# One-hot rows compared from PSUM, weight low parts all on GpSimd, 72 instead of 56 early chunks, and gathered rows paced into the last group

## The chip, the cores and the metric

One core of a Trainium2 chip runs one launch of the kernel. The metric is the device time of that launch in microseconds (us), the median of the runs shown; lower is better. The engines are TensorE (PE; PEld is its weight load), VectorE (DVE), ScalarE (ACT), GpSimd (POOL) and the DMA queues, which SyncE (SP), ACT and POOL issue. TensorE has a granted clock with two levels, 2.4 GHz (1.0 in the profile) and 1.2 GHz (0.5).

## The reference

One decoder layer on 512 tokens of width 2048: pooling mixer and dilated attention, cross attention over 256 memory tokens, then the part that this change is mostly about, PEER, a product-key mixture of 16384 single-neuron experts:

```
q = hf @ w_pq                                  # 8 heads x 2 halves of 128
s1, s2 = halves of q against 128 sub-keys each
v1, i1 = top_k(s1, 16);  v2, i2 = top_k(s2, 16)
sc, ci = top_k(all sums v1 + v2, 16)           # 16 of 256 candidates
experts = i1[ci // 16] * 128 + i2[ci % 16];  gates = softmax(sc)
a = hf . w_u[experts];  y = sum over experts of gates * gelu(a) * w_v[experts]
out = rmsnorm(x + y)
```

## The kernel before, in words

**Precision.** Each f32 weight tile of 128x1024 is split into two fp32r parts: a high part `wh` (a cast on ACT, L143) and a low part `wl = raw - wh` (L144, on DVE or on POOL, by the argument `lo_eng`). Three matmuls (`mm3`, L150 to L152) make one product. Both parts have three buffers, the raw tile four.

**Two ways through PEER.** For the last 320 tokens all 16384 experts are computed densely, as 128 chunks of 128 experts; a matrix of gates, zero where an expert was not picked, multiplies them. For the first 192 tokens only the picked experts' rows are gathered: 128 tokens ("dot0", "axpy0", 128 rows each) and 64 middle tokens (packed as 2x64, "dot1", "axpy1", 64 rows each). Each row is one indirect DMA on POOL (L114; 128 partitions x 8 KB, 1 MB) and one DVE operation over 2048 elements with the other operand or the sum in PSUM. These 389 steps stand in one list; `behind(n)` pops n of them at a time, `n` being a rate (`RATE`) per chunk. Row buffers are four at most in the stages of interest.

**Stages from the pick on.** (a) The pick, for three blocks of 128 tokens (`pick_steps`, L263): candidate sums, top 16, and per head a one-hot over 50 candidates for 16 slots: compare (L293), multiply by the expert number (L295), reduce (L296), all on DVE. Its result is transposed by PE (L1054 to L1056) into `e12T` and `gT`. After each block `a_until` computes seven early chunks of h @ w_u with a gelu; they go to DRAM (`gad`). (b) The gates: for four tokens at a time (80 blocks), `gates` makes two one-hots of 128 (L1114), multiplies one by the gate (L1116), one PE product per token makes the 128x128 gate matrix (L1119), ACT copies it to a 2 MB stage (L1120). These run between early chunks 21 to 55. (c) The 16 groups of 8 chunks, each 16 output tiles `dd` of 24 matmuls: group g multiplies the gated chunks with w_v and adds to `xT` (L1193), while `c_chunk` makes the 8 chunks of the next group. The 9 late groups (chunks 56 to 127) compute their chunks there; the 7 early groups come last and load theirs from DRAM.

```
1023        lo = G if j < RB * KB else (V, G) if j < K1 else G if j < K1 + GRP or j % 2 == 0 else V
1053            pt = pa.tile([P, 512], F32, name="pa")
1054            TE.transpose(pt[:, 0:P], e12[:, 0, :], ident)
1061            a_until(KB * b + KB)
1114            V.tensor_tensor(u, iota.unsqueeze(1).unsqueeze(1).broadcast_to([P, 2, 4, P]),
1115                            e12T[:, :, t:t + 4].unsqueeze(3).broadcast_to([P, 2, 4, P]), op=ALU.is_equal)
1116            V.tensor_tensor(u[:, 1], u[:, 1], gT[:, t:t + 4].unsqueeze(2).broadcast_to([P, 4, P]), op=ALU.mult)
1117            pg = pa.tile([P, 4, P], F32, name="pa")
1119                TE.matmul(pg[:, j], u[:, 0, j], u[:, 1, j], start=True, stop=True)
1120            S.copy(stage[:, :, t4 * 4:t4 * 4 + 4].rearrange("p e t -> p t e"), pg)
```

**What sets the order.** A scheduler orders each engine's instructions ahead of time by priority and its own time model; an engine then runs them strictly in that order. POOL follows the program's order from the gates on (L1065). `issue_after` keeps a gathered row behind the last DVE split (`anchor`, L159). In PSUM the pool `pa` has two banks.

**Earlier.** Attention begins (L753 on) with the rotary tables: positions are loaded, `trig` makes `sinT` and `cosT` (L764 to L767), and `rope` (L771) applies them to each head's q and k on POOL.

Of the kernel before, what the change touches and what calls it, by code (L numbers as in the profile page):

```python
# [9 lines left out]
F32 = mybir.dt.float32  # L10
# [7 lines left out]
P = 128  # L18
# [3 lines left out]
KD = D // P  # L22
# [20 lines left out]

RATE = (3.0, 2.2, 2.5, 2.0, 0.25, 1.2)

# [3 lines left out]

K1, U0, GE = 56, 0, 2  # L50

KB = 7

# [10 lines left out]
def hybrid_kernel(ctx: ExitStack, tc: tile.TileContext, a: dict, out: bass.AP):  # L64
# [28 lines left out]
    r2c = const.tile([P, TR], F32, name="r2c")  # L93
    rz = const.tile([P, NB], F32, name="rz")[:, :RB]
    accx = const.tile([P, TR], F32, name="accx")
    xT = big.tile([P, KD, TR], F32, name="xT")
    x0 = big.tile([P, D], F32, name="x0")
# [37 lines left out]
    def load_w(src, lo_eng=None, parts=1):  # L135
# [11 lines left out]
        return wh, wl  # L147

    def mm3(ps, wh, wl, xh, xl, start, stop):
        TE.matmul(ps, wh, xh, start=start, stop=False)  # L150
        TE.matmul(ps, wh, xl, start=False, stop=False)  # L151
        TE.matmul(ps, wl, xh, start=False, stop=stop)  # L152

# [108 lines left out]

    def pick_steps(vals, inds, alloc, res):  # L263
        v1, v2 = vals[:, 0], vals[:, 1]
# [24 lines left out]
        eid = alloc([P, PH, 16], name="eid")  # L289
        ohs = [alloc([P, 16, NCAND], name="oh%d" % i) for i in range(2)]  # L290
# [15 lines left out]

    def pick(vals, inds, alloc):
        res = []
        for _ in pick_steps(vals, inds, alloc, res):
            pass  # L310
        return res
# [52 lines left out]
    v0 = kt.tile([P, HEADS, P], F32, name="v0")  # L364
    halo = kt.tile([P, 8, 16], F32, name="halo")

    def alloc_ma():
# [7 lines left out]
    with tc.tile_pool(name="ep", bufs=1) as ep, tc.manual_schedule(engines={mybir.EngineType.SP}):  # L375
# [269 lines left out]
        def xr_sq(k):  # L645
            sumsq(lambda n: ep.tile([P, TR], F32, name="jk", bufs=2), accx, xT[:, k, :], k == 0, TR)
# [63 lines left out]
        for k in range(KD):  # L710
            hooks_x[k // 8][k % 8] = [lambda k=k: xr_sq(k)]
        for g in range(4):
# [29 lines left out]
    def pick0():  # L742
        res = []
        yield from pick_steps(vals0, inds0, lambda shape, name, dt=F32: (mA if name in ("oh0", "oh1") else m2)(shape, dt=dt), res)
        V.tensor_copy(sidx, res[0])
        V.tensor_copy(sgate, res[1])
# [6 lines left out]
    with tc.tile_pool(name="ac", bufs=1, reuse_waits="tile") as ac, tc.tile_pool(name="at", bufs=2, reuse_waits="tile") as at:  # L753
        tmp2k = lambda n=TR, dt=F32: at.tile([P, T], dt, name="t2k", bufs=3)[:, :n]
        mask = ac.tile([P, T], F32, name="mask")
        nc.scalar.dma_start(mask, a["mask"])
        invf = ac.tile([32, 1], F32, name="invf")
        nc.scalar.dma_start(invf, a["invfreq"])
        cosT = ac.tile([32, TR], F32, name="cosT")
        sinT = ac.tile([32, TR], F32, name="sinT")  # L760
        posi = tmp2k(TR, I32)[:32]
        nc.scalar.dma_start(posi, a["positions"][:, T0:].broadcast_to([32, TR]))
        ang = tmp2k()[:32]
        V.tensor_copy(ang, posi)  # L764
        V.tensor_scalar(ang, ang, scalar1=invf, scalar2=None, op0=ALU.mult)
        trig(ang, tmp2k()[:32], sinT, cosT)
        V.tensor_scalar(sinT[0:16], sinT[0:16], scalar1=-1.0, scalar2=None, op0=ALU.mult)  # L767
        rx = r2c
# [252 lines left out]
    def a_chunk(j, stay=False):  # L1021

        lo = G if j < RB * KB else (V, G) if j < K1 else G if j < K1 + GRP or j % 2 == 0 else V
        ps = proj_one(a["w_u"][j], dH, dL, ND, lo_eng=lo, rate=RATE[4] if j < RB * KB else RATE[5] if j < K1 else 0)
# [12 lines left out]
    with tc.tile_pool(name="tw", bufs=1, reuse_waits="tile") as tw:  # L1037
        for b in range(RB):
            eidf, gtf = pick(vals[:, b], inds[:, b], lambda shape, name, dt=F32: tw.tile(shape, dt, name=name))
            ei = tw.tile([P, 2, PH * 16], I32, name="ei")  # L1040
# [13 lines left out]
            TE.transpose(pt[:, 0:P], e12[:, 0, :], ident)  # L1054
            TE.transpose(pt[:, P:2 * P], e12[:, 1, :], ident)
            TE.transpose(pt[:, 2 * P:3 * P], gtf, ident)  # L1056
# [37 lines left out]
    with tc.tile_pool(name="gw", bufs=2, side="right", reuse_waits="tile") as gw:  # L1094
        for k4 in range(4):
            pt = pa.tile([P, 512], F32, name="pa")
            for kk in range(4):
                k = 4 * k4 + kk
                hn = gw.tile([P, SG, NS], F32, name="hn0")
                for g in range(SG):  # L1100
                    V.scalar_tensor_tensor(out=hn[:, g, :], in0=xT[:, k, :NS], scalar=gains[:, 3, k:k + 1], in1=r2c[:, :NS], op0=ALU.mult, op1=ALU.mult)
                TE.transpose(pt[:, kk * P:(kk + 1) * P], hn.rearrange("p g t -> p (g t)"), ident)
            S.copy(hy1[:, k4 * 512:(k4 + 1) * 512], pt)

        stage = None

        def gates(i):
            nonlocal stage
            tb, t4 = divmod(i, 8)
            if t4 == 0:  # L1110
                stage = gw.tile([P, P, 32], F32, name="stage", bufs=1)
            u = gw.tile([P, 2, 4, P], F32, name="u", bufs=3)
            t = i * 4
            V.tensor_tensor(u, iota.unsqueeze(1).unsqueeze(1).broadcast_to([P, 2, 4, P]),  # L1114
                            e12T[:, :, t:t + 4].unsqueeze(3).broadcast_to([P, 2, 4, P]), op=ALU.is_equal)
            V.tensor_tensor(u[:, 1], u[:, 1], gT[:, t:t + 4].unsqueeze(2).broadcast_to([P, 4, P]), op=ALU.mult)  # L1116
            pg = pa.tile([P, 4, P], F32, name="pa")
            for j in range(4):
# [18 lines left out]
    with tc.tile_pool(name="vg", bufs=2, side="right", reuse_waits="tile") as vg, \  # L1137
# [30 lines left out]
        cs = []  # L1168
        slots = (NG - 1) * KD - 4
        n2 = NCH - K1  # L1170
# [3 lines left out]
        for jj in range(GRP):  # L1174
            cs.append(c_chunk(GRP * order[0] + jj))
            behind(RATE[5])
        fin = None
        for i, g in enumerate(order):
# [8 lines left out]
            for dd in range(KD):  # L1187
# [8 lines left out]
                behind(rate2 if i < n2 // GRP - 1 else rate3)  # L1196
                if last:
                    if dd == KD - 2:
                        S.activation(warm, accf[:, 0:1], AF.Sqrt)
                    sumsq(ftmp, accf, xT[:, dd, NS:], dd == 0, ND, eng=V)  # L1200
                    S.activation(xT[:, dd, NS:], xT[:, dd, NS:], AF.Copy, scale=gains[:, 4, dd:dd + 1])
            if i == NG - 2:
                behind(1000)
                for k4 in range(4):
                    pt = pa.tile([P, 512], F32, name="pa")
                    for kk in range(4):
                        TE.transpose(pt[:, kk * P:(kk + 1) * P], y1[0][:, (4 * k4 + kk) * P:(4 * k4 + kk + 1) * P], ident)
                    o = xT[:, 4 * k4:4 * k4 + 4, :NS]
                    for sg_ in range(SG):
                        V.tensor_tensor(o, pt.rearrange("p (k g t) -> p k g t", k=4, t=NS)[:, :, sg_, :], o, op=ALU.add)  # L1210
                for k in range(KD):
                    sumsq(ftmp, accs, xT[:, k, :NS], k == 0, NS)
                    S.activation(xT[:, k, :NS], xT[:, k, :NS], AF.Copy, scale=gains[:, 4, k:k + 1])
            cs = nxt
# [100 lines left out]
```

## Time and profile before

| | |
|---|---|
| three runs | 3178.96, 3163.85, 3175.17 us; median 3175.17 |
| the profiled execution | 3175.37 us, span 3173.6 us |
| mean granted clock | 0.968 |
| busy share of the span | PE 93%, DVE 76%, POOL 45%, ACT 41% |
| DMA | 912.79 MB, mean 288 GB/s |
| last gathered row issued | 3005 us into the span |

A busy PE is not a PE at its peak, since matmuls overlap; so PE's work is counted here in matmuls and their start-to-start time. All stretches are microseconds from the start of the span. The stage of picks, early chunks and gates lies at 1146 to 1690; the groups' windows, cut at the first addition of each group, run from 1749 to 3152.

### The profile page before, as it was taken

What the parts mean: (1) busy time and instruction counts of PE and PEld (TensorE: products, weight loads), DVE (VectorE), ACT (ScalarE), POOL (GpSimd) and SP (SyncE); (2) the same over time, 40 slices, a digit from 0 to 9 for tenths busy, and PEclk for the clock granted to TensorE, in tenths of its full rate; (3) what the DMA queues carried; (4) which work ended last, traced back from release to release, by engine and by line L of the source; (5) the groups of instructions that cost most, each with busy time, mean ns of one, the idle gap of its engine ahead of it and who ended that gap; (6) DMA issues with size and microseconds to landing.
All of it is one profiled execution on the core that took longest, in us unless ns stands there. A gap on an engine that the chain in (4) does not pass through costs nothing.

```text
span 3173.6 us, 47405 instructions
## 1 busy us (share of the span) xinstructions
PE 2947.7 (93%) x18311; PEld 2832.5 (89%) x18311; DVE 2422.7 (76%) x3360; ACT 1298.6 (41%) x1789; POOL 1433.8 (45%) x826
## 2 busy tenths in 40 slices
PE   7999879998988997899998999999999999999997
PEld 5868769988978997899998999999999999899997
DVE  7797877798878579599894767777777678787756
ACT  5676534432344443355543333333433333233334
POOL 0000046644534665544546555555555554454532
PEclk9999989999989998999999999999999999999998
DMA  7886737888975344588888989999899999999953
GB/s 261 295 300 214 244 119 282 330 309 339 342 266 192 111 127 124 182 302 318 315 304 315 357 325 359 357 367 355 330 372 353 353 354 358 346 357 362 343 163 106
DMA packets 243521, 912.79 MB, mean 288 GB/s; under 512 B 23488, under 2 KB 85600, under 8 KB 192224
## 3 DMA queue, kind: packets, MB, share of 16 engines
q1 hardware_dynamic: 136304, 471.21, 42.2%
q0 software_dynamic: 55296, 402.68, 32.1%
q10 hardware_dynamic: 51696, 35.88, 3.7%
q8 instruction: 144, 2.36, 0.3%
q14 instruction: 81, 0.66, 0.1%
HBM read 874.22 MB, written 35.45 MB: 287 GB/s over the span
## 4 chain that ended last, share of the span: by engine, by line
PE 66%; DVE 20%; DMA 5%; issue 5%; ACT 2%; POOL 0%; ACTq 0%; POOLq 0%; DVEq 0%; SPq 0%
PE pm L150 11%; PE pm L152 11%; PE pm L151 11%; PE pa L152 9%; PE pa L150 9%; PE pa L151 9%; DVE wl L144 2%; DVE u L1114 2%; DVE oh L295 1%; DVE oh L293 1%; PE pm L400 1%; PE pm L401 1%; PE pm L399 1%; PE pa L1119 1%; DMA rows<-in_w_v_rows_dram,sidx 1%
## 5 line engine op out<-in xcount | busy, mean ns | idle before, releaser
L144 POOL TENSOR_TENSOR wl<-wraw,wh 128x1024 fp32r<-128x1024 f32 x369 | 930.5, 2526 | 1433.3 <-ACT wh L143 1401.4
L143 ACT ACTIVATE wh<-wraw 128x1024 fp32r<-128x1024 f32 (+1 forms) x658 | 693.7, 1058 | 1042.1 <-PE pm L151 467.0
L152 PE MATMUL pa<-ch,wl 128*128 128x320 f32 x2048 | 634.5, 312 | 25.4 <-DVE wl L144 23.5
L150 PE MATMUL pm<-dH,wh 128*128 128x320 f32 x2048 | 640.4, 313 | 15.0 <-DVE cl L1164 6.5
L152 PE MATMUL pm<-dH,wl 128*128 128x320 f32 x2048 | 640.6, 313 | 6.1 <-DVE wl L144 3.9
L150 PE MATMUL pa<-ch,wh 128*128 128x320 f32 x2048 | 636.7, 311 | 7.3 <-DVE xT L1193 4.7
L151 PE MATMUL pm<-dL,wh 128*128 128x320 f32 x2048 | 639.0, 312 | 0.0
L151 PE MATMUL pa<-cl,wh 128*128 128x320 f32 x2048 | 635.3, 310 | 0.0
L144 DVE TENSOR_TENSOR wl<-wraw,wh 128x1024 fp32r<-128x1024 f32 (+1 forms) x289 | 377.4, 1308 | 166.5 <-ACT wh L143 158.7
L152 PEld LDWEIGHTS pa<-ch,wl 128*128 128x128 f32 x2048 | 387.1, 189 | 30.4 <-DVE wl L144 28.1
L150 PEld LDWEIGHTS pm<-dH,wh 128*128 128x128 f32 x2048 | 389.2, 190 | 16.3 <-DVE cl L1164 6.8
L150 PEld LDWEIGHTS pa<-ch,wh 128*128 128x128 f32 x2048 | 388.3, 190 | 10.2 <-ACT ch L1163 5.2
L152 PEld LDWEIGHTS pm<-dH,wl 128*128 128x128 f32 x2048 | 389.3, 190 | 8.2 <-DVE wl L144 5.4
L151 PEld LDWEIGHTS pm<-dL,wh 128*128 128x128 f32 x2048 | 389.3, 190 | 0.0
L151 PEld LDWEIGHTS pa<-cl,wh 128*128 128x128 f32 x2048 | 388.1, 190 | 0.0
L150 PE MATMUL pm<-hH,wh 128*128 128x384 f32 x1024 | 355.9, 348 | 10.4 <-DVE k L811 3.4
L152 PE MATMUL pm<-hH,wl 128*128 128x384 f32 x1024 | 354.2, 347 | 10.5 <-DVE wl L144 10.5
L151 PE MATMUL pm<-hL,wh 128*128 128x384 f32 x1024 | 354.4, 346 | 5.2 <-DVE hL L874 4.4
L1193 DVE TENSOR_TENSOR xT<-pa,xT 128x320 f32<-128x320 f32 x256 | 124.7, 487 | 196.6 <-PE pa L152 191.0
L150 PEld LDWEIGHTS pm<-hH,wh 128*128 128x128 f32 x1024 | 197.6, 193 | 17.1 <-issue 5.8
L152 PEld LDWEIGHTS pm<-hH,wl 128*128 128x128 f32 x1024 | 197.6, 193 | 13.4 <-DVE wl L144 12.5
L151 PEld LDWEIGHTS pm<-hL,wh 128*128 128x128 f32 x1024 | 197.7, 193 | 6.9 <-DVE hL L874 4.7
(413 smaller groups left out, 4571.6 us busy)
## 6 DMA issues: line engine op xcount, KB each, us to landing
wraw<-in_w_u_dram SPq DMA_DIRECT2D x256, 512.0 KB
wraw<-in_w_v_dram SPq DMA_DIRECT2D x256, 512.0 KB
wraw<-in_w_in_dram SPq DMA_DIRECT2D x64, 512.0 KB
xT<-in_w_in_f_dram SPq DMA_DIRECT2D x63, 512.0 KB
gd<-stage SPq DMA_DIRECT2D x10, 2048.0 KB
gt<-gd ACTq DMA_DIRECT2D x32, 640.0 KB
wraw<-in_w_pq_f_dram SPq DMA_DIRECT2D x32, 512.0 KB
wraw<-in_w_out_dram SPq DMA_DIRECT2D x32, 512.0 KB
```

Of the source, the lines that this page charges most:

```text
L143: S.activation(wh[:, c], raw[:, c], AF.Copy)
L144: i = (lo_eng or V).tensor_tensor(wl[:, c], raw[:, c], wh.bitcast(F32)[:, c], op=ALU.subtract)
L150: TE.matmul(ps, wh, xh, start=start, stop=False)
L151: TE.matmul(ps, wh, xl, start=False, stop=False)
L152: TE.matmul(ps, wl, xh, start=False, stop=stop)
L293: V.tensor_tensor(oh, iota50.unsqueeze(1).broadcast_to([P, 16, NCAND]), cf[:, h, :].unsqueeze(2).broadcast_to([P, 16, NCAND]), op=ALU.is_e ...
L295: V.tensor_tensor(oh, oh, ecand[:, h, :].unsqueeze(1).broadcast_to([P, 16, NCAND]), op=ALU.mult)
L399: TE.matmul(ps, xh, wh, start=start, stop=False)
L400: TE.matmul(ps, xh, wl, start=False, stop=False)
L401: TE.matmul(ps, xl, wh, start=False, stop=stop)
L1114: V.tensor_tensor(u, iota.unsqueeze(1).unsqueeze(1).broadcast_to([P, 2, 4, P]), e12T[:, :, t:t + 4].unsqueeze(3).broadcast_to([P, 2, 4, P] ...
L1193: V.tensor_tensor(xT[:, dd, NS:], ps[:, :ND], xT[:, dd, NS:], op=ALU.add)
```

## The change

The diff, cut to what acts (all its parts are here):

```diff
-RATE = (3.0, 2.2, 2.5, 2.0, 0.25, 1.2)
+RATE = (3.0, 2.2, 2.5, 2.0, 0.25, 0.9, 1.4)
-K1, U0, GE = 56, 0, 2
-KB = 7
+K1, U0, GE = 72, 0, 2
+QE, QA = 7, 9
+KB = 10
...
-    def pick_steps(vals, inds, alloc, res):
+    def pick_steps(vals, inds, alloc, res, eng=V, bank=None):
...
+        if bank is not None:
+            io, oh = bank[:, :NCAND], bank[:, NCAND:9 * NCAND].rearrange("p (s c) -> p s c", c=NCAND)
+            V.tensor_copy(io, iota50)
...
+            if bank is not None:
+                for s in range(0, 16, 8):
+                    V.tensor_tensor(oh, io.unsqueeze(1).broadcast_to([P, 8, NCAND]),
+                                    cf[:, h, s:s + 8].unsqueeze(2).broadcast_to([P, 8, NCAND]), op=ALU.is_equal)
+                    V.tensor_tensor(oh, oh, ecand[:, h, :].unsqueeze(1).broadcast_to([P, 8, NCAND]), op=ALU.mult)
+                    V.tensor_reduce(eid[:, h, s:s + 8], oh, axis=AX.X, op=ALU.add)
...
-            V.tensor_tensor(oh, oh, ecand[:, h, :].unsqueeze(1).broadcast_to([P, 16, NCAND]), op=ALU.mult)
+            eng.tensor_tensor(oh, oh, ecand[:, h, :].unsqueeze(1).broadcast_to([P, 16, NCAND]), op=ALU.mult)
...
-        yield from pick_steps(vals0, inds0, ..., res)
+        yield from pick_steps(vals0, inds0, ..., res, G)
...
+        hooks_x[2][0] = [pos_in]        # two DMAs on ACT's queue: positions, invfreq
+        hooks_x[2][5] = [trig_rows]     # the same trig, into cosT (kt pool) and sinT (= accx[:32])
...
-        (mask's stage: invf, posi loads, V.tensor_copy, V.tensor_scalar, trig, sign of sinT)
...
-        lo = G if j < RB * KB else (V, G) if j < K1 else G if j < K1 + GRP or j % 2 == 0 else V
-        ps = proj_one(..., rate=RATE[4] if j < RB * KB else RATE[5] if j < K1 else 0)
+        lo = G if j < K1 + GRP or j % 2 == 0 else V
+        ps = proj_one(..., rate=RATE[5] if j < RB * KB else RATE[6] if j < K1 else 0)
...
-            eidf, gtf = pick(vals[:, b], inds[:, b], ...)
+            eidf, gtf = pick(vals[:, b], inds[:, b], ..., pa.tile([P, 512], F32, name="pa"))
...
+            a_until(KB * b + KB)
             pt = pa.tile([P, 512], F32, name="pa")
-            TE.transpose(...) x3
+            with tc.issue_after(last_mm[0].ins):
+                TE.transpose(...) x3
...
-            a_until(KB * b + KB)
...
+                hx = gw.tile([P, NS], F32, name="hx0")
+                G.tensor_tensor(hx, xT[:, k, :NS], r2c[:, :NS], op=ALU.mult)
                 for g in range(SG):
-                    V.scalar_tensor_tensor(out=hn[:, g, :], in0=xT[:, k, :NS], scalar=gains[:, 3, k:k + 1], in1=r2c[:, :NS], op0=ALU.mult, op1=ALU.mult)
+                    S.activation(hn[:, g, :], hx, AF.Copy, scale=gains[:, 3, k:k + 1])
...
+        io, pg = (pa.tile([P, 4, P], F32, name="pa") for _ in range(2))
+        V.tensor_copy(io, iota.unsqueeze(1).broadcast_to([P, 4, P]))
...
-            V.tensor_tensor(u, iota..., e12T..., op=ALU.is_equal)
-            V.tensor_tensor(u[:, 1], u[:, 1], gT..., op=ALU.mult)
-            pg = pa.tile([P, 4, P], F32, name="pa")
+            V.tensor_tensor(u[:, 0], io, e12T[:, 0, t:t + 4].unsqueeze(2).broadcast_to([P, 4, P]), op=ALU.is_equal)
+            for j in range(4):
+                V.tensor_scalar(u[:, 1, j], io[:, j], scalar1=e12T[:, 1, t + j:t + j + 1], scalar2=gT[:, t + j:t + j + 1],
+                                op0=ALU.is_equal, op1=ALU.mult)
...
-        slots = (NG - 1) * KD - 4
+        slots = (NG - 1) * KD + QE - 2
...
-            behind(RATE[5])
+            behind(RATE[6])
...
                 if last:
+                    if dd == QE:
+                        behind(1000)
+                    if QA <= dd < QA + 4:
+                        (4 transposes of y1, 2 additions to xT, 4 sumsq and 4 scalings: a quarter of the block below)
...
-            if i == NG - 2:
-                behind(1000)
-                (16 transposes of y1, 8 additions to xT, 16 sumsq and 16 scalings)
```

In the gate stage `io` and `pg` now take both banks of `pa`, so the gate products share one bank where they rotated over two.

## Rows read from the trace of the kernel before

**Rows 1.** The page, part 1: busy time, share of the span, instructions of each engine.
```profile
PE 2947.7 (93%) x18311; PEld 2832.5 (89%) x18311; DVE 2422.7 (76%) x3360; ACT 1298.6 (41%) x1789; POOL 1433.8 (45%) x826
```

**Rows 2.** By stretch: length, busy PE PEld DVE ACT POOL (instructions), clock, DMA, GB/s.
```profile
1146.00:1690.00 544.00, 493.97 (x3391) 486.86 (x3391) 477.12 (x642) 236.25 (x271) 284.10 (x122) 0.95 0.70 251
2000.00:2080.00 80.00, 80.00 (x548) 80.00 (x547) 57.65 (x50) 28.50 (x35) 42.86 (x26) 1.00 0.94 358
1749.30:2662.70 913.40, 904.21 (x6125) 902.37 (x6125) 662.94 (x630) 324.38 (x394) 489.72 (x295) 0.99 0.92 352
2662.70:2977.40 314.70, 293.25 (x1923) 287.48 (x1922) 248.46 (x256) 99.82 (x121) 157.05 (x93) 0.98 0.94 352
2977.40:3040.20 62.80, 58.22 (x394) 57.43 (x393) 48.25 (x54) 22.54 (x28) 26.09 (x14) 1.00 0.80 295
3040.20:3098.90 58.70, 56.65 (x385) 55.52 (x384) 26.22 (x53) 23.02 (x49) 18.83 (x8) 1.00 0.50 153
```

**Rows 3.** What PE waited for, 1146 to 1690: us in total, times, longest.
```profile
PE pa L1054 <- DVE e L1052: 20.8, 3, 11.0
PE pa L1119 <- DVE u L1116: 14.7, 11, 3.6
PE pm L150 <- ACT wh L143: 5.7, 2, 3.1
...
PE pa L1119 <- ACT stage L1120: 2.1, 1, 2.1
```

**Rows 4.** PE in order of time at one gate block: start, us, instruction, idle before.
```profile
1395.52 1.28 PE L1119 MATMUL pa<-u 128*128 128x128 f32 x10
1396.56 0.39 PE L150 MATMUL pm<-dH,wh 128*128 128x320 f32 x1
```

**Rows 5.** Costliest DVE groups, 1146 to 1690: count, busy us, mean ns, idle before.
```profile
L1114 DVE TENSOR_TENSOR u<-iota,e12T 128x1024 f32<-128x1024 f32 x80 | 119.9, 1517 | 0.7 <-PE pa L1119 0.7
L1116 DVE TENSOR_TENSOR u<-u,gT 128x512 f32<-128x512 f32 x80 | 72.4, 917 | 0.3
L144 DVE TENSOR_TENSOR wl<-wraw,wh 128x1024 fp32r<-128x1024 f32 x35 | 46.9, 1340 | 31.1 <-ACT wh L143 31.1
L295 DVE TENSOR_TENSOR oh<-oh,ecand 128x800 f32<-128x800 f32 x24 | 45.3, 1922 | 0.0
L293 DVE TENSOR_TENSOR oh<-iota,cf 128x800 f32<-128x800 f32 x24 | 40.4, 1717 | 0.0
L331 DVE SCALAR_TENSOR_TENSOR gx<-rows,sact,gx 128x2048 f32<-128x2048 f32 x12 | 28.2, 2349 | 12.4 <-DMA rows<-in_w_v_rows_dram,sidx 12.4
L296 DVE TENSOR_REDUCE eid<-oh 128x16 f32<-128x800 f32 x24 | 22.6, 971 | 0.0
```

**Rows 6.** Durations of single lines on DVE, min/median/max ns, first and last start.
```profile
L1114 DVE TENSOR_TENSOR u<-iota,e12T x80: 1208/1212/3437, 1291.7 to 1665.6; 128x1024 f32<-128x1024 f32 x80
L1193 DVE TENSOR_TENSOR xT<-pa,xT x256: 469/491/494, 1749.3 to 3151.3; 128x320 f32<-128x320 f32 x128
L208 DVE TENSOR_SCALAR rd<-ident,rz x3: 272/281/289, 365.3 to 371.2; 128x128 f32<-128x128 f32 x3
```

**Rows 7.** POOL: durations of its splits; then its row gathers (x) in two stretches.
```profile
L144 POOL TENSOR_TENSOR wl<-wraw,wh x369: 2345/2411/6655, 376.7 to 3141.8; 128x1024 fp32r<-128x1024 f32 x185
...
440.00:1690.00 1250.00, 175.71 (x151) 0.96 0.71 256
1146.00:1690.00 544.00, 59.74 (x43) 0.95 0.70 251
```

**Rows 8.** Where the first rotary step is waited for: PE's row; then the stretch.
```profile
411.68 1.22 PE L818 MATMUL pa<-kT,q 128*128 128x128 f32 x4 [13.33 <-POOL q L776]
...
398.00:430.00 32.00, 13.20 (x49) 10.98 (x47) 31.97 (x123) 8.81 (x16) 6.17 (x7) 0.63 0.12 34
```

**Rows 9.** What PE waited for, 2662.7 to 3040.2 (groups with loaded chunks).
```profile
PE pa L152 <- DVE wl L144: 16.8, 14, 2.3
```

**Rows 10.** The copy of a gate block to the stage, as a group of the lines view.
```profile
L1120 ACT COPY stage<-pa 128x512 f32<-128x512 f32 x80 | 86.2, 1117 | 71.6 <-PE pa L1119 53.3 <-DMA gd<-stage 17.9
```

More of the change, by code (lines that the diff above doesn't have):

```diff
@@ L94, in hybrid_kernel @@
     rz = const.tile([P, NB], F32, name="rz")[:, :RB]
+    invf = const.tile([32, 1], F32, name="invf")
     accx = const.tile([P, TR], F32, name="accx")
+    sinT = accx[:32]
     xT = big.tile([P, KD, TR], F32, name="xT")
@@ L151, in mm3 @@
         TE.matmul(ps, wh, xl, start=False, stop=False)
-        TE.matmul(ps, wl, xh, start=False, stop=stop)
+        last_mm[0] = TE.matmul(ps, wl, xh, start=False, stop=stop)
     def proj_one(tiles, xh, xl, n=TR, lo_eng=None, rate=0):
@@ L289, in pick_steps @@
         eid = alloc([P, PH, 16], name="eid")
-        ohs = [alloc([P, 16, NCAND], name="oh%d" % i) for i in range(2)]
-        for h in range(PH):
+        if bank is not None:
+            io, oh = bank[:, :NCAND], bank[:, NCAND:9 * NCAND].rearrange("p (s c) -> p s c", c=NCAND)
+            V.tensor_copy(io, iota50)
+        else:
+            ohs = [alloc([P, 16, NCAND], name="oh%d" % i) for i in range(2)]
+        for h in range(PH):
+            if bank is not None:
[4 more added lines that the diff above has]
+                    V.tensor_reduce(eid[:, h, s:s + 8], oh, axis=AX.X, op=ALU.add)
+                yield
+                continue
             oh = ohs[h % 2]
@@ L305, in pick_steps, with pick @@
         res.extend((eid.rearrange("p h k -> p (h k)"), gt.rearrange("p h k -> p (h k)")))
-    def pick(vals, inds, alloc):
+    def pick(vals, inds, alloc, bank):
         res = []
-        for _ in pick_steps(vals, inds, alloc, res):
+        for _ in pick_steps(vals, inds, alloc, res, bank=bank):
             pass
@@ L365, in hybrid_kernel @@
     halo = kt.tile([P, 8, 16], F32, name="halo")
+    cosT = kt.tile([32, TR], F32, name="cosT")
     def alloc_ma():
@@ L711, in hybrid_kernel, with pos_in, trig_rows @@
             hooks_x[k // 8][k % 8] = [lambda k=k: xr_sq(k)]
+        posr = []
+        def pos_in():
+            posr.append(ep.tile([P, TR], F32, name="jk", bufs=2)[:32].bitcast(I32))
+            nc.scalar.dma_start(posr[0], a["positions"][:, T0:].broadcast_to([32, TR]))
+            nc.scalar.dma_start(invf, a["invfreq"])
+        def trig_rows():
+            V.tensor_copy(cosT, posr[0])
+            V.tensor_scalar(cosT, cosT, scalar1=invf, scalar2=None, op0=ALU.mult)
+            trig(cosT, ep.tile([P, TR], F32, name="jk", bufs=2)[:32], sinT, cosT)
+            V.tensor_scalar(sinT[0:16], sinT[0:16], scalar1=-1.0, scalar2=None, op0=ALU.mult)
+        hooks_x[2][0] = [pos_in]
+        hooks_x[2][5] = [trig_rows]
         for g in range(4):
@@ L743, in pick0 @@
         res = []
-        yield from pick_steps(vals0, inds0, lambda shape, name, dt=F32: (mA if name in ("oh0", "oh1") else m2)(shape, dt=dt), res)
+        yield from pick_steps(vals0, inds0, lambda shape, name, dt=F32: (mA if name in ("oh0", "oh1") else m2)(shape, dt=dt), res, G)
         V.tensor_copy(sidx, res[0])
@@ L756, in hybrid_kernel @@
         nc.scalar.dma_start(mask, a["mask"])
[L757 to L767, printed above, removed]
         rx = r2c
@@ L1021, in a_chunk @@
     def a_chunk(j, stay=False):
[L1023 to L1024 removed]
+        lo = G if j < K1 + GRP or j % 2 == 0 else V
+        ps = proj_one(a["w_u"][j], dH, dL, ND, lo_eng=lo, rate=RATE[5] if j < RB * KB else RATE[6] if j < K1 else 0)
         ga = ps[:, :ND] if stay else apool.tile([P, ND], F32, name="ga")
@@ L1038, in hybrid_kernel @@
         for b in range(RB):
-            eidf, gtf = pick(vals[:, b], inds[:, b], lambda shape, name, dt=F32: tw.tile(shape, dt, name=name))
+            eidf, gtf = pick(vals[:, b], inds[:, b], lambda shape, name, dt=F32: tw.tile(shape, dt, name=name),
+                             pa.tile([P, 512], F32, name="pa"))
             ei = tw.tile([P, 2, PH * 16], I32, name="ei")
@@ L1197, in hybrid_kernel @@
                 if last:
+                    if dd == QE:
+                        behind(1000)
+                    if QA <= dd < QA + 4:
+                        k4 = dd - QA
+                        pt = pa.tile([P, 512], F32, name="pa")
+                        for kk in range(4):
+                            TE.transpose(pt[:, kk * P:(kk + 1) * P], y1[0][:, (4 * k4 + kk) * P:(4 * k4 + kk + 1) * P], ident)
+                        o = xT[:, 4 * k4:4 * k4 + 4, :NS]
+                        for sg_ in range(SG):
+                            V.tensor_tensor(o, pt.rearrange("p (k g t) -> p k g t", k=4, t=NS)[:, :, sg_, :], o, op=ALU.add)
+                        for k in range(4 * k4, 4 * k4 + 4):
+                            sumsq(ftmp, accs, xT[:, k, :NS], k == 0, NS)
+                            S.activation(xT[:, k, :NS], xT[:, k, :NS], AF.Copy, scale=gains[:, 4, k:k + 1])
                     if dd == KD - 2:
@@ L1201, in hybrid_kernel @@
                     S.activation(xT[:, dd, NS:], xT[:, dd, NS:], AF.Copy, scale=gains[:, 4, dd:dd + 1])
-            if i == NG - 2:
-                behind(1000)
[L1204 to L1213, printed above, removed]
             cs = nxt
```

10 lines of the change are left out of this document (4 added, 6 removed).

## The prediction

> **What bounds the kernel now.** The page says that PE is busy for 93% of the span [rows 1], so the question is in which stretches PE falls short of its own pace, and who keeps it waiting. The pace: in an undisturbed stretch 548 matmuls of 320 columns fill 80 us, 0.146 us each [rows 2]. Against it I count each stage.
>
> *Picks, early chunks, gates (544 us).* 56 chunks of 48 matmuls are 2688 x 0.146 = 392 us. Ten gate matmuls take 1.04 us from the first one's start to the next matmul's [rows 4], so the 80 blocks of eight cost 80 x 0.83 = 66. The other 63 matmuls [rows 2] add 7. That is 465, so 79 us are lost. The table of waits names DVE first [rows 3]: 20.8 us in three waits for the pick's result ahead of its transposes, and 14.7 us in eleven waits for the gates' one-hots. The granted clock is 0.95 there [rows 2], some 0.05 x 544 = 27 us more in stretches at 1.2 GHz, which follow such idle times. DVE is busy for 477 of the 544 us.
>
> Why DVE is that full is seen in single durations. The compare of 1024 elements takes 1.21 us at best and 3.44 at worst, 1.52 in the mean; the 800-element ones have means of 1.72 and 1.92 where the reduce of the same size takes 0.97 [rows 5, 6]. The excess of the worst, 2.2 us, is one POOL split (2.41 us) [rows 7]. The addition that reads one operand from PSUM stays between 0.469 and 0.494 us in all 256 cases, though POOL splits run beside it [rows 6]. So what reads both operands from SBUF waits for POOL, and what reads one from PSUM does not.
>
> *Groups.* Eight windows in which late chunks are computed take 913.4 us for 6144 x 0.146 = 897: 2 us lost in each. Five windows with loaded chunks take 314.7 us for 5 x 384 x 0.146 = 280: 6.9 us lost in each. The two after them, with few or no gathered rows, take 62.8 and 58.7 instead of 56.1 [rows 2]. What PE waits for in these is DVE's low part, 14 times [rows 9].
>
> *Start of attention.* PE idles 13.3 us for the first rotary product, in a 32 us stretch at a clock of 0.63 in which DVE is never idle [rows 8].
>
> **The change part by part.**
>
> *One-hots from PSUM.* From 0.49 us for 320 elements out of PSUM [rows 6], at one element a cycle, 400 elements cost about 0.58 and 512 about 0.70. A pick's head becomes 2 x 3 operations of at most 0.58, 3.5 us, instead of 1.92 + 1.72 + 0.97 = 4.6. A gate block becomes 0.70 and four scalar operations of 128, for which the nearest row gives 0.28 each [rows 6]: 1.8 us instead of 1.52 + 0.92 = 2.4 [rows 5]. Unknown is whether a PSUM source costs a scalar operation more: between 0.13 (128 cycles) and 0.49 (the 320-element row), so 1.2 to 2.7 a block; I take 1.8.
>
> *Low parts on POOL.* 35 DVE splits (47 us [rows 5]) become POOL splits of 2.41, and the first-token products (`hx`) move to POOL and ACT, some microseconds each. DVE's load in the stage: 477 less 24 x 1.1 (picks), 80 x 0.6 (gates), 47 (splits) and 9 (`hn`), plus 43 more gathered rows at 2.35 [rows 5], 101: about 447 us in some 600, 75% instead of 88%. POOL: 144 splits x 2.41 and 86 gathers x 1.4 (59.7 us for 43 [rows 7]), 467 of 600, 78% instead of 52%.
>
> *Transposes behind ten chunks instead of none.* A pick (eight heads of 3.5 and a top 16, about 42 us, with nine rows 63) now has ten chunks, 70 us, to finish under. The 20.8 us go; next late would be the third pick, with 7 us to spare. The 14.7 us for one-hots go with DVE's load. These two are 35.5 of the 43.3 us in [rows 3], so I give them 82% of the clock's 27: 57.5 us removed, 21.5 left. The 16 chunks that move here bring 112 us of work that a later stage loses, and 4% of it, 4 us, for the loss that remains. **Early stage: -54.**
>
> *Fewer computed, more loaded windows.* Two windows change kind. Computed ones: six instead of eight at 2 us, **-4.** For loaded ones the rows count. The program's rates give 149 steps before the groups (151 gathers by 1690 [rows 7]); the new ones 27 instead of 5 in the picks and 59 instead of 42 after them, 188. So 201 steps are left of 389 instead of 240, over 245 slots instead of 236. The first rate falls from 1.32 to 1.07 a tile, but the second stays: (201 - 1.07 x 96) / 149 = 0.66 against 0.655. Loaded windows thus are as crowded as before and there are nine: eight with rows at 6.9 and one, where the list ends, at about 3.5, 59 us lost instead of 34.4 + 6.7 + 2.6 = 44. **+15**, between -20 (all at 2.6) and +18 (all at 6.9).
>
> *Rotary tables earlier.* The most to be had is 32 us less PE's 13.2 busy ones at half clock, about 23; nothing, if the next product waits on DVE just as long, which has no idle time there. In the new place ten DVE operations of at most 0.5 us (by the 0.49 row) go between splits. I take 13.3 less 4: **-9.** The two small loads on ACT's queue move ahead by five tiles. The multiply of the first pick goes to POOL at 2.41 x 800/1024 = 1.9 us, eight times; POOL is busy for 6 of those 32 us [rows 8].
>
> *Last group.* Since the list ends in the fifteenth window, no row runs on into the last. The sums of the middle tokens lie beside 24 matmuls a tile; DVE's and ACT's shares rise in four tiles and ACT has three to catch up. 0, between -2.6 (the loss of the window that they leave) and +5.
>
> **Sum:** 3175.4 - 54 - 4 + 15 - 9 = 3123 us. The profiled execution (3175.37) stands at the median of the runs (3175.17), so nothing is to be shifted.
>
> **The rivals.**
>
> *POOL becomes the bound.* In the stage POOL takes every split and every gather in program order, and a gather waits at the queue's head until DVE has freed its buffer. If each waited for one more DVE operation (2.35), a chunk would cost POOL 4.82 + 0.9 x 3.75 = 8.2 us in the picks against 7.0 on PE, and 4.82 + 1.4 x 3.75 = 10.1 against 8.7 in the gates: 30 x 1.2 + 42 x 1.4 = 95 us, less the slack of three buffers. I price it at 65: 3188 us. Against it: with 43 gathers [rows 7] at a DVE load of 88%, PE has no POOL wait among its larger ones [rows 3]. The Trainium skill (GPSIMD Engine Reference, Engine selection) says that element by element work on two inputs belongs on VectorE, GpSimd being about twice as slow. By that rule the splits should have stayed, and the trace agrees on the ratio, 2.41 us [rows 7] against the 1.21 of DVE's undisturbed 1024-element operation [rows 6]. Chance 0.09.
>
> *One bank for the gates' products* is the way to slower. A block's products must now wait until ACT has copied the block before (1.12 us [rows 10]), where two banks let them run ahead. If PE's order puts blocks back to back, each wait costs that copy: 80 x 1.12 = 90 us, 3213. It decides if fewer than eight matmuls (1.12/0.146) stand between two blocks. For it: before, pairs of blocks did run together (ten gate matmuls in a row [rows 4]). Against: the scheduler knows the bank and can put a chunk's 48 matmuls between. Chance 0.08.
>
> *DMA fills up in the gate stage.* A chunk brings 1 MB of weights, 1.4 MB of rows, 0.16 of `gad` and half a MB of stage, 3.2 million bytes in 8.7 us: 365 GB/s. The windows that lose little ran at 352 and 358 [rows 2]. At 345 it is 0.5 us more for 40 chunks: 3143. Chance 0.12.
>
> *The change does not do what it says:* DVE is held by POOL even with a PSUM operand. Then DVE's holds stay, its load is again 88%, and the 14.7 us with their clock share of 9 stay: 3147. Against it the 256 even durations [rows 6]. Chance 0.05.
>
> **How the numbers follow.** My forecast has 0.66. Its low end is all 79 us of the early stage, 15 at the rotary step and loaded windows that lose 10 less: 3085. Its high end is 3147 to 3165, with the two milder rivals and no gain at the rotary step. 3085 to 3165 leaves out the first two rivals, 0.17. About 0.5%, 16 us, is what a measurement of this kernel can tell: the forecast and the two milder rivals are faster (0.83), POOL's rival falls within (0.09), the bank's is slower (0.08).
>
> **What would show it.** Right: no wait of PE on the transposes; compares at 0.7 us with no long ones; the stage of 72 chunks in about 600 us at a clock of 0.98; loaded windows still at 62 to 63 us with DVE splits ahead of PE. Wrong: PE waiting for POOL's low parts or ACT's stage copy, a DMA share of 0.97 in the gates, or loaded windows near 58.

## The result and the profile after

The changed kernel takes 3197.24 us (median of seven runs, 3193.15 to 3198.53) beside 3178.96 for the kernel before: a ratio of 1.0061, 95% interval 1.0041 to 1.0081. It is slower by 0.6%, where 3123 and faster were forecast. The profiled execution took 3196.82 us, its span is 3195.1. One of the six runs of experiment 2 below took 4111.63 us at a granted clock of 0.65 and is left out of its ratio.

To see where, I count in every trace what PE loses: the sum, over its instructions, of start-to-start time beyond the usual one for that tile (the median, 0.147 us for 320 columns, 0.176 for 384, 0.111 for 128), so a lower clock counts as loss too. PE's work is the same in all kernels, 2825 us. In us, by stage:

```
                                          before   after
up to the last score (rotary tables)       190.0   179.3
picks and early chunks, to the 1st gate     41.8    12.7
gates, to group 0's first addition          36.3    71.7
groups 0 to 13                              50.8    71.2
last two groups and the end                  8.8    14.2
sum                                        327.7   349.1
```

The first stage came out as forecast. The picks won 29 us, the gates lost 35, and the groups lost another 20. The windows view (length, busy time and instructions of PE, PEld, DVE, ACT, POOL, then clock, DMA share, GB/s) has the same in rows, against [rows 2]: the picks, the gates, their tail, the first six computed windows, the loaded ones.

```profile
1131.00:1344.00 213.00, 209.72 (x1427) 208.39 (x1425) 134.73 (x445) 83.01 (x105) 139.24 (x59) 1.00 0.53 167
1344.00:1752.00 408.00, 385.26 (x2652) 377.64 (x2653) 277.78 (x428) 182.68 (x233) 273.06 (x161) 0.97 0.86 326
1752.00:1856.00 104.00, 72.96 (x447) 70.71 (x446) 46.45 (x62) 31.21 (x42) 43.26 (x25) 0.79 0.65 247
1856.00:2536.00 680.00, 677.68 (x4613) 676.37 (x4612) 444.19 (x444) 246.42 (x298) 352.40 (x198) 1.00 0.86 320
...
2598.00:2994.00 396.00, 357.58 (x2319) 350.42 (x2318) 304.33 (x320) 120.55 (x148) 193.63 (x113) 0.97 0.91 337
```

In the picks PE is hardly held up and the clock is 1.00; in the 104 us after the early chunks PE is busy for 73 at a clock of 0.79, and no engine is full. On the page DVE fell from 76% to 72% and POOL rose from 45% to 48%, against [rows 1]:

```profile
PE 2952.3 (92%) x18311; PEld 2828.6 (89%) x18311; DVE 2309.3 (72%) x3585; ACT 1305.4 (41%) x1822; POOL 1536.6 (48%) x901
```

PE's waits (us in total, times, longest), against [rows 3]: the first line is from 1131 to 1344, the next two from 1344 to 1752, the last two from 1752 to 1856. Those for the picks' transposes and for the one-hots are gone; the copy to the stage stands in their place:

```profile
PE pm L158 <- POOL wl L148: 1.9, 1, 1.9
...
PE pa L1148 <- ACT stage L1149: 17.3, 14, 4.3
PE pa L1129 <- ACT hn L1128: 3.1, 7, 0.7
...
PE pa L1148 <- ACT stage L1149: 17.4, 7, 10.7
PE pm L156 <- DVE cl L1193: 13.6, 1, 13.6
```

The one-hots did what was forecast: even durations, no long ones (min/median/max ns), against [rows 6].

```profile
L1143 DVE TENSOR_TENSOR u<-pa,e12T x80: 683/692/709, 1352.4 to 1782.3; 128x512 f32<-128x512 f32 x80
L1145 DVE TENSOR_SCALAR u<-pa,e12T,gT x320: 401/405/432, 1353.0 to 1783.8; 128x128 f32<-128x128 f32 x160
```

What happens in the tail is read from the chain that ended last (start, us, what), from 1754 on:

```profile
1755.55 1.02 ACT stage L1149
1756.59 12.83 DMA gd<-stage
1769.52 1.02 ACT stage L1149
1770.59 2.09 PE pa L1148 x8
1772.69 1.04 ACT stage L1149
1773.78 2.09 PE pa L1148 x8
...
1791.83 1.02 ACT stage L1149
1792.87 6.26 DMA gd<-stage
1799.20 4.60 DMA gt<-gd
1803.90 0.51 DVE pm L1188
```

A full stage is written out (12.83 us), the next copy waits for that write, then seven gate blocks run one after the other, 3.19 us each, with no chunk between them; the last stage goes out, comes back as `gt`, and only then can group 0 be prepared. All this should lie beside the chunks. Counting PE's gate matmuls at the stores of the early chunks shows where it goes wrong: the blocks fall behind, a little at each stage that fills up (the count stands at 17, 25, 33, 41, 49, 57 and 65 while one to three chunks go by).

```
gate blocks (of 80) done at the store of chunk   31    41    51    61    71
after                                           3.0  18.0  33.0  52.8  69.0
after, two stage buffers (e1)                   3.0  23.0  42.5  65.5  80.0
after, two banks, SBUF one-hots (e2)            4.0  23.8  42.0  66.0  80.0
after, issued earlier (e4)                      3.8  19.5  33.0  49.8  69.0
```

### The profile page after: what moved, and what is told of

Read it like the earlier page. It is cut to its first block, busy times and chain, and to the rows that moved or that the text cites. A ratio compares the mean times of both kernels' runs of the same rounds, so it can differ in the third digit from the quotient of the medians.

```text
span 3195.1 us, 47813 instructions
## 1 busy us (share of the span) xinstructions
PE 2952.3 (92%) x18311; PEld 2828.6 (89%) x18311; DVE 2309.3 (72%) x3585; ACT 1305.4 (41%) x1822; POOL 1536.6 (48%) x901
## 4 chain that ended last, share of the span: by engine, by line
PE 71%; DVE 14%; DMA 6%; issue 4%; ACT 3%; POOL 1%; ACTq 0%; SPq 0%; DVEq 0%; POOLq 0%
PE pm L156 13%; PE pm L158 13%; PE pm L157 12%; PE pa L158 8%; PE pa L156 8%; PE pa L157 8%; PE pa L1148 3%; DVE wl L148 2%; DVE rows L336 1%; PE pm L419 1%; PE pm L420 1%; DVE wl L134 1%; PE pm L418 1%; DMA rows<-in_w_u_rows_dram,sidx 1%; DVE hL L223 1%
## 5 line engine op out<-in xcount | busy, mean ns | idle before, releaser
L148 POOL TENSOR_TENSOR wl<-wraw,wh 128x1024 fp32r<-128x1024 f32 x420 | 1024.4, 2441 | 1374.8 <-ACT wh L147 1323.0
L148 DVE TENSOR_TENSOR wl<-wraw,wh 128x1024 fp32r<-128x1024 f32 (+1 forms) x238 | 312.3, 1313 | 139.1 <-ACT wh L147 137.0
```

Of the source, the lines that this page charges most:

```text
L148: i = (lo_eng or V).tensor_tensor(wl[:, c], raw[:, c], wh.bitcast(F32)[:, c], op=ALU.subtract)
```

## The experiments

Each experiment was timed beside the kernel before on the same chip (its median there: 3178.52 us for experiments 1 to 4, 3176.39 for 5 to 8, 3174.49 for 9 to 12). Between these three groups the ratios to the kernel before compare better than the times.

**1. Two stage buffers.** The theory with which I began (B below) was the single bank by itself; the standstills at the full stages gave the rival, S.

```diff
-                stage = gw.tile([P, P, 32], F32, name="stage", bufs=1)
+                stage = gw.tile([P, P, 32], F32, name="stage", bufs=2)
```

> The changed kernel with two stage buffers in place of one; the gates' products keep their single PSUM bank. In the changed kernel the last of the 80 gate blocks ends 48 us after the last gelu of chunk 71, and 113 us go by between that gelu and the start of group 0's products (59 us before the change); the first copy after every full stage stands behind that stage's 2 MB write. Theory S (the single stage stops the single bank's chain at each of the turnovers, some one to one and a half chunks each, and nothing catches up): the lag of the blocks behind the chunks goes, the last block falls before the last gelu, 113 us go to some 60, about 3145 us (3130 to 3160). Theory B (the single bank alone: each block's one-hots, products and copy in series, whatever the stage does): blocks still slip, at least 5 are left over after chunk 71, 3175 to 3200 us. Theory G (GpSimd or the DMA engines are full in this stage): as the changed kernel, 3190 to 3200 us.

Measured 3148.31 us, ratio to before 0.9904 (0.9882 to 0.9925). The last block starts at 1702, before chunk 71's store at 1740; from that store to group 0's first addition it is 66 us instead of 112. Copies no longer wait for the write, PE waits 5.9 us for them in place of 34.7 (the tile's view, after and e1):

```profile
  PE pa L1148: 34.7, 21
  ACT stage L1149: 15.1, 4
```
```profile
  PE pa L1148: 5.9, 8
```

S holds, B and G fall: with one bank and two stages nothing slips.

**2. Two banks, one stage.**

```diff
-        io, pg = (pa.tile([P, 4, P], F32, name="pa") for _ in range(2))
-        V.tensor_copy(io, ...)
...
+            V.tensor_tensor(u, iota..., e12T..., op=ALU.is_equal)
+            V.tensor_tensor(u[:, 1], u[:, 1], gT..., op=ALU.mult)
+            pg = pa.tile([P, 4, P], F32, name="pa")
```

> The changed kernel with the gate blocks' one-hots as before the change (two operations, counting row in SBUF) and the products going over two PSUM banks in turn; one stage buffer as in the changed kernel. Theory B (the single bank is what the blocks slip by): the blocks keep up, the tail after the last gelu falls from 113 to some 60 us, and TensorE waits for GpSimd holding VectorE's copies come back, so some 3150 us (3135 to 3170). Theory S (the single stage alone): the turnovers still cost a chunk or more each, at least 4 blocks left over, 3175 us or more. Theory G: no change, 3190 to 3200 us.

Measured 3167.45 us, 0.9961 (0.9941 to 0.9981). The blocks keep up here too, so S in its strict form falls: the single stage alone makes nothing slip. It takes the one bank and the one stage together. A copy that waits for the stage's write leaves the other bank free for the next block; with one bank everything behind it stands still. But the gates still lost 64.5 us. The largest wait there is for the one-hots:

```profile
PE pa L1146 <- DVE u L1143: 28.4, 15, 4.2
PE pa L1146 <- ACT stage L1147: 2.9, 4, 1.3
```

With the same one-hots, one bank and two stages (experiment 6) that wait is 8.6 us and the gates lose 40.4, so the one-hots are not all of it. What a single stage costs there beside two banks stays open.

**3. The kernel before with one bank.**

```diff
+        _, pg = (pa.tile([P, 4, P], F32, name="pa") for _ in range(2))
...
-            pg = pa.tile([P, 4, P], F32, name="pa")
```

> The kernel before with a single change: the gate blocks' products all go to one PSUM bank (the other one is left unused). Theory B, and S, which needs both the one bank and the one stage: 2.4 blocks are issued per chunk and at most two can be turned round, so more than 20 of the 80 blocks are left after chunk 55, each some 3.2 us with nothing beside it; 60 to 90 us slower than before, 3240 to 3270 us. Theory G: within 10 us of the kernel before.

Measured 3257.29 us, 1.025 (1.022 to 1.028): 79 us for the bank, in a kernel in which nothing else was changed. By the trace 65 us lie in the gates (101.5 lost for 36.3) and 16 in the groups. At the store of chunk 55, the last one, 53 of the 80 blocks are done; between 1660 and 1815 PE waits for the rest:

```profile
PE pa L1119 <- ACT stage L1120: 41.4, 23, 8.0
PE pm L150 <- DVE cl L1164: 13.4, 1, 13.4
```

**4. Blocks issued earlier.**

```diff
-K1, U0, GE = 72, 0, 2
+K1, U0, GE = 72, 0, 12
```

> The changed kernel, in which the gate blocks are issued so that the last one is due 12 chunks before the end of the run of chunks rather than 2 (80 blocks over 30 chunks instead of 40); all else as changed. If blocks are late only because they are issued late (theory L), the tail after the last gelu falls from 113 to about 60 us and the time to some 3145 us. Theories B and S: a block that is issued earlier waits all the same for the bank and the stage, so the last block ends where it did, 3190 to 3200 us.

One run: 3175.16 us. The blocks stand at 69 after chunk 71 as before, and the same 13.4 us wait for the first gated chunk follows, so L falls. The time is 20 us below what B and S expected; by the trace 14 of them lie in the gates (57.6 lost for 71.7; 24.5 us of waits for the copy in place of 34.7) and the rest behind them. That I had not foreseen, and it is one run.

**5. Rows moved out of the loaded windows** (on e1).

```diff
-R2 = 1.3
+R2 = 1.9
```

> The kernel of e1_stage2 with 1.9 in place of 1.3 as the factor by which GpSimd's queue of gathered rows runs faster in the six computed windows than on the average (some 24 rows in each, 5 left for a loaded window, where e1_stage2 has 16 to 19 and 9 to 12). In e1_stage2 the products of the loaded windows wait 39 us for VectorE's low parts (26 waits of 1.5 us), and the computed windows lose next to nothing. Theory P (VectorE stands still while GpSimd holds the port for a row's products, so rows that run in a loaded window delay its low parts): the 39 us fall to some 15 to 20, and the computed windows, which have VectorE to spare, stay at 113 us each: 3125 to 3138 us. Theory W (a loaded window waits for its weights' transfers, whatever the rows do): within 5 us of e1_stage2's 3148. Theory C (the rows only move the cost): the computed windows grow by what the loaded ones lose, 3140 to 3160.

Measured 3189.30 us, 1.0033 (1.0016 to 1.0051), 41 us slower than e1. The loaded windows did win, 19 us lost instead of 72, but the computed ones lost 99 instead of 3. One window of each kind, first e5 (computed, loaded), then e1 (computed, loaded):

```profile
2182.00:2318.00 136.00, 119.08 (x770) 118.03 (x769) 97.63 (x100) 39.28 (x49) 69.28 (x43) 0.94 0.88 336
...
2643.00:2700.00 57.00, 54.95 (x372) 54.36 (x371) 37.49 (x46) 19.84 (x24) 23.07 (x15) 1.00 0.79 284
```
```profile
2256.00:2369.00 113.00, 112.53 (x767) 112.26 (x766) 71.98 (x82) 39.21 (x49) 58.93 (x33) 1.00 0.87 318
...
2547.00:2611.00 64.00, 60.28 (x392) 58.70 (x391) 50.47 (x63) 17.68 (x22) 29.80 (x18) 0.97 0.92 341
```

A loaded window with six rows takes 57 us and one with ten 64: the rows are what delays it, as theory P has it and W has not, though no run here shows that the held port is the way in which they do. For the kernel as a whole theory C holds, and beyond its numbers. POOL's group of `rows` gathers (busy, mean | idle before, by releaser), in e5 and in e1 from 1800 to the end, shows a part of what breaks in the computed ones: at 23 to 26 rows a window the gathers wait at the head of POOL's queue for DVE to free a buffer.

```profile
L118 POOL DMA_INDIRECT rows<-in_w_v_rows_dram,sidx x60 | 65.0, 1084 | 48.9 <-DVE gx L349 32.3 <-DVE gx L1111 7.4 <-issue 5.2
```
```profile
L118 POOL DMA_INDIRECT rows<-in_w_v_rows_dram,sidx x60 | 64.1, 1069 | 10.4 <-issue 5.3 <-DVE sact L1104 0.2
```

What TensorE waits for in e5's computed windows (1917 to 2580) is not GpSimd's low parts but VectorE's. How the late gathers and the added row operations on VectorE share in that was not tried further.

```profile
PE pa L158 <- DVE wl L148: 67.7, 18, 6.0
```

**6 and 7. The one-hots back in SBUF**, in the gates and in the picks (on e1).

```diff
-            (one compare and four scalar operations from io in PSUM)
+            (one compare and one multiplication from iota in SBUF, as before)
```
```diff
-                             pa.tile([P, 512], F32, name="pa"))
+                             None)
```

> The kernel of e1_stage2 (two stages, one bank for the products) with the gate blocks' one-hots as before the change, two operations with the counting row in SBUF. In e2_two_banks, with these one-hots, TensorE waited 28.4 us for them, in 15 places. Theory H (VectorE's holds behind GpSimd's gathers are what the counting row in PSUM frees): those waits come back, 15 to 40 us more than e1_stage2, 3163 to 3188 us. Theory N (with the stage doubled the slack covers them): within 8 us of e1_stage2's 3148.

> The kernel of e1_stage2 with the picks' one-hots from SBUF as before the change; ten chunks per block of tokens and the transposes behind the last of them stay. Theory T (what freed the pick stage is that the transposes stand behind the chunks, not where the one-hots are): 30 chunks of 7.05 us still hide a pick even when GpSimd's products hold VectorE up, within 6 us of e1_stage2's 3148. Theory H2 (the holds lengthen a pick of some 65 us beyond its ten chunks of 70 us): TensorE waits 10 to 20 us at each of the three transposes but the first, 3165 to 3190 us.

Measured 3158.11 us (0.9938, 0.9917 to 0.9960) and 3166.30 us (0.9946, 0.9923 to 0.9969): 10 and 18 us more than e1 (11 and 13 by the ratios; e7's five runs lie 20 us apart, and its trace is of the slowest). In e6 the waits for one-hots come back only in part (8.6 us, four times). In time, 10 us is below the 15 that H asked for and above the 8 that N allowed; by the trace the gates lose 40.4 us instead of 21.9, within H's range, and the groups, where the two programs are the same, happen to lose 10 less. In e7 the picks lose 33 us instead of 14. H2 had the price but not the place: PE waits 9.6 us for ACT's high parts and 4.8 for POOL's low parts, not at the transposes. GpSimd is slowed too, as its groups show, low parts and gathers, e6 and then e1 in the gate stage:

```profile
L148 POOL TENSOR_TENSOR wl<-wraw,wh 128x1024 fp32r<-128x1024 f32 x77 | 193.8, 2520 | 62.8 <-ACT wh L147 60.5 <-PE pa L1146 1.0
L118 POOL DMA_INDIRECT rows<-in_w_v_rows_dram,sidx x28 | 42.9, 1532 | 16.7 <-DVE gx L349 12.9 <-issue 1.9 <-PE pm L158 0.2
```
```profile
L148 POOL TENSOR_TENSOR wl<-wraw,wh 128x1024 fp32r<-128x1024 f32 x76 | 182.5, 2403 | 108.1 <-ACT wh L147 107.9
L118 POOL DMA_INDIRECT rows<-in_w_v_rows_dram,sidx x27 | 25.7, 953 | 4.0 <-issue 1.2 <-DVE u L1145 0.2 <-PE pm L158 0.2
```

The Trainium skill (SBUF — State Buffer, section "SBUF: two separate sides") says that VectorE's operations with two inputs in SBUF and GpSimd's share a pair of ports under an exclusive lock. The rows of the low parts agree from GpSimd's side (2.52 us for 2.40), as [rows 6] did from VectorE's.

**8. 64 early chunks** (on e1).

```diff
-K1, U0, GE = 72, 0, 2
+K1, U0, GE = 64, 0, 2
-KB = 10
+KB = 8
```

> The kernel of e1_stage2 with 64 early chunks, eight per block of tokens, in place of 72 and ten (24 beside the picks, 40 beside the gates, 7 computed windows and 8 loaded ones after the first). A loaded window of e1_stage2 loses some 8 us more than a computed one, and eight chunks last 56 us beside a pick of some 65. Theory E (every early chunk beside the picks is won, 7 us each where a pick outlasts its chunks): the pick stage loses 3 times 8 us, the loaded windows gain 8: 3155 to 3168. Theory D (the extra loaded window costs as much as the extra early chunks win): 3143 to 3153. Below 3143 would say that 72 is too many.

Measured 3138.25 us, 0.9862 (0.9836 to 0.9888), 10 us below e1 (13 by the ratios): 72 is too many. The picks lose 16 us instead of 14, so with the row in PSUM a pick fits under eight chunks too; groups 0 to 13 lose 54 instead of 75. The time shows less than these 21 us because this trace loses 10 more than e1's ahead of the picks, where the programs are the same.

**9. The kernel before with two stages**, the diff of the first experiment.

> The kernel before with one change: two stage buffers in place of one. It has two banks for the gates' products, so a copy that waits at a turnover doesn't stop the blocks behind it, and it can turn round more than the 2.4 blocks per chunk that are issued. If it takes the one bank and the one stage together to make blocks slip (theory S): little to win, 3168 to 3182 us. If the stage alone costs a turnover's wait whatever the banks (theory St): the 28 us that TensorE lost between the first gate block and the last fall by 15 or more, 3155 to 3165 us.

Measured 3191.66 us, 1.0058 (1.0041 to 1.0076): slower. For the gates S was right, they lost 32 us instead of 36. The 17 us came in the groups (73 lost instead of 51), where the two kernels are the same but for what the stage had left behind. From 1745 to 2560 PE's wait for DVE's low parts is longer (before, then e9):

```profile
PE pa L152 <- DVE wl L144: 6.7, 3, 3.0
```
```profile
PE pa L152 <- DVE wl L144: 22.7, 6, 5.5
```

Four of the eight windows lose 4 to 13 us each in e9, two of them 5 to 7 in the kernel before. Why these windows, which carry 19 to 22 rows each in both kernels, fell over there stays open; it was not tried further.

**10 and 11. The norm's transposes beside the picks** (on e8), and 1.45 for `R2` with it.

```diff
+            if b > 0:
+                for k4 in (2 * b - 2, 2 * b - 1):
+                    (hx on POOL, hn on ACT, four transposes, copy to hy1)
...
-        for k4 in range(4):
-            (the same)
```

> The kernel of e8_k64 with the norm's 16 transposes and their copies moved from between the picks and the gates to beside the picks (two of the four at the start of the second pick, two at that of the third). In e8_k64 TensorE lost 9.5 us between the first of these transposes and the first gate block, beside some 2 us of work. If those waits are what it costs (theory A): 8 to 12 us faster than e8_k64, 3126 to 3132. If a pick has no time to spare beside eight chunks (theory F): they come back at the picks' transposes, 3134 to 3142.

> The kernel of e10_hn_early with 1.45 in place of 1.3 as the factor of the gathered rows in the computed windows. At 1.9 (e5_rows_earlier) the loaded windows lost 19 us in place of 72, and the computed ones 98 in place of 2. If the loss starts well above the 16 to 19 rows per computed window of 1.3 (theory K, a knee): one or two rows fewer in each loaded window win some 2 us apiece, 10 to 20 us faster than e10_hn_early. If it rises from there on (theory R, no room): 5 to 25 us slower than e10_hn_early.

Measured 3117.63 us (0.9818, 0.9801 to 0.9835) and 3115.81 us (0.9814, 0.9796 to 0.9832). Both beat both kernels, the one before by 1.8 and 1.9%. Picks and gates lose 30 us in e10 and 38 in e8: 8 us for the move, theory A. The other 12 or so are not the move's; 9 us lie ahead of the picks, where the two programs are the same. In e11 the windows up to the eighth lose 23 us instead of 8.5 and those after it, to the fourteenth, 30 instead of 40: neither K nor R; in these two traces the rows' cost rises from 1.3 on and only changes place.

**12. The rotary tables put back** (on e8).

```diff
-        hooks_x[2][0] = [pos_in]
-        hooks_x[2][5] = [trig_rows]
...
+        (loads, trig and sign at the start of the attention, as before)
```

> The kernel of e8_k64 with the rotary tables where they were before the change, at the start of the attention. The prediction put the move at 9 us, by TensorE's wait of 13.3 us for the tables' chain. If it holds: 6 to 13 us slower than e8_k64's 3138, with that wait of some 13 us back between the last scores of the 128 tokens and the first products of the attention. If something else ends that wait (the keys' rotation on GpSimd itself): within 4 us.

Measured 3139.55 us, 0.9889 (0.9867 to 0.9911), 1.3 us from e8's time. But the two ran on different chips, and by the ratios e12 is 0.0027 slower, some 9 us, known to about 11 either way: the times alone decide nothing. The wait is back, and what e8 has in its place is nearly as long (e12, then e8, 335 to 480):

```profile
PE pa L834 <- POOL q L792: 12.7, 1, 12.7
PE pa L835 <- POOL k L792: 3.7, 1, 3.7
```
```profile
PE pa L841 <- DVE t2k L845: 8.2, 2, 6.6
PE pa L842 <- POOL k L799: 5.0, 1, 5.0
```

From 330 to the last score e8 loses 129 us and e12 135; over all traces it is 119 to 129 us in the ten with the tables moved and 132 to 137 in the four without. So over all traces the move is worth some 11 us up to the last score; this pair, with e8 the worst of the ten, shows 6 there.

## Why the prediction was wrong

**What failed: the single bank was priced by its copy, and the single stage at nothing.** In the prediction's terms one bank makes each block wait for a copy of 1.12 us, which lies beside a chunk's matmuls, and the stage is half a MB for the DMA engines. No term has the two together. [rows 10] shows the wait: ACT idle for 17.9 us in front of the copy until `gd<-stage` had landed. With two banks that idle time was covered (e9: the second stage is worth 4 us in the gates there); with one, the copy that waits for the 2 MB write stops the blocks behind it (e1: 49 us of the changed kernel's 3197, 49 of the 74 us between forecast and measurement).

**The rival at 0.08 had the place and the sign, not the mechanism.** "One bank for the gates' products" was priced at 3213, 80 copies with blocks back to back, and 3197 came; that the two are near is luck. Its condition, fewer than eight matmuls between two blocks, is met in 17 of the 79 gaps of the changed kernel, 7 of them in the tail. The argument against it, that the scheduler "can put a chunk's 48 matmuls between", came true: the commonest gap is 24 matmuls, two blocks a chunk (37 gaps, and 49 in e1). With two stages that is enough (e1). With one, little is left to catch up with after a standstill, as the change issues two blocks a chunk; issuing 2.67 left the same 69 of 80 done at the store of chunk 71 (e4).

**Early stage: -54 forecast, +6 measured** (picks and gates together, 78.1 lost before, 84.4 after). With the stage doubled it is -42, and with 64 chunks and the norm's transposes moved -48 (e10). So the mechanism of the term was right and its size near. A part of the rest is the `hx` and `hn` step, put at "some microseconds each" with no place: between the picks and the gates TensorE has nothing else, and 11 us were lost from 1343 to 1365. The counting row in PSUM does its part: by the traces 18 us in the gates and 19 in the picks (e6, e7), in time 10 and 13 to 18. Its scalar operations cost 0.34 us each from start to start (107.6 us for 316 in e1), not the 0.28 taken from an SBUF row; a block 2.05 us rather than 1.8, inside the bounds. The Trainium skill (VectorE: DVE Perf Modes, "Why PSUM operands drop a tier") says that a PSUM operand denies f32 its faster mode; these rows agree in direction (a single one lasts 0.40 us, the SBUF row's 0.28), though the SBUF row has one scalar and these have two.

**Groups: -4 and +15 forecast, +20 measured.** The +15 was too small. With the fifteenth window, which the table counts at the end, nine loaded windows lose 74.7 us for the seven of before 40.4: +34, beyond the +18 set as the most. The six computed ones lose 3 for the eight's 13: -10. The loaded ones took 64.9 us each (eight, 2536 to 3055.5), not the 62 to 63 of [rows 2]. "As crowded as before" held for the rows (9 to 12 a window, 10 or 11 before), but the losses are by the rows (at 5 or 6 a window e5 loses 19 us from the seventh window to the fourteenth, e1 72), and e8, with one loaded window fewer, loses 21 us less in groups 0 to 13. Why ten rows cost more here than in the kernel before stays open.

**Rotary tables: -9 forecast, -10.7 measured** up to the last score, 11 over all traces (experiment 12). The wait of [rows 8] went and shorter ones came.

**Last group: 0 forecast, +5.4 measured** after the fourteenth window. Of these 2.1 lie in the last window and go with the moved sums: it loses 7.7 to 8.3 us in all eleven kernels that have them and 5.8 in the three that do not, within the forecast's bounds. The other 3.3 are the fifteenth window, above; six of the eleven lose less than 1 us there. What the rest lose there stays open.

**The other rivals.** POOL is not the bound: PE waited for its low parts once, for 1.9 us, in the picks. The DMA share in the gates is 0.86, not 0.97. DVE is free with a PSUM operand, as the 692 ns show. The range's high end was also added up too low: 3123 with both milder rivals (20 and 24) and without the rotary step's 9 is 3176, not 3165; 3197 lies outside either.

By the table's stages, the terms that missed, 60 early, 9 in the groups and 5 at the end, less 2 at the tables, are 72 of the 74 us between 3123 and 3197.

## What to carry to other kernels

A buffer that goes from two to one is priced together with every other single buffer on the same round trip: look for the longest wait anywhere in that loop (here a 2 MB write), not only for the step beside the buffer. Then ask how many turns per unit of covering work the loop can make and how many are issued; where they are equal, as here, the standstills can add up and come out at the end, uncovered. A row of idle time that costs nothing today says what may be exposed when the cover goes.

## What the runs showed that I had not expected

GpSimd's gathers are slowed by VectorE's work on SBUF as its arithmetic is: issuing one took 1.53 us beside SBUF one-hots and 0.95 beside PSUM ones. Over all traces, computed windows lost at most 3 us each at 15 to 18 rows, between nothing and 13 at 19 to 22, and some 20 at 23 to 26 (five of e5's six), though in e5 the DMA engines were no busier (0.88 for 0.87). And two builds whose programs agree up to the picks can differ by 9 us there (e8 and e10), as much as several of the effects looked for; stage by stage, over many traces, such effects can still be told.
